# S5 input products as two 96-row matmuls a block, their operands stacked by DMA through DRAM

## The chip, the cores and the metric

The kernel runs on one core of one Trainium2 chip. Its engines are TensorE (PE in the profile, with weight loads as PEld), VectorE (DVE), ScalarE (ACT), GpSimd (POOL) and SyncE (SP); each works through its own queue in order. The metric is device time in microseconds (us), lower is better. Before the change it is 1423.0 us, the median of 3 runs (1422.8 to 1423.98).

## The reference

One decoder block on 256 tokens of width 2048, in float32. After a norm, one large projection (2048 to 9216) feeds two token mixers; gates merge them; a gated MLP with a short convolution follows. The change touches the S5 mixer alone:

```python
uf = u.reshape(bsz, L, 64, 16)                      # 64 groups of 16 channels
abar = exp(lam_re*dt) * (cos(lam_im*dt) + i sin(lam_im*dt))
bu_re = einsum('blgc,gpc->blgp', uf, b_re)          # 16 channels -> 64 states, per group
bu_im = einsum('blgc,gpc->blgp', uf, b_im)
bb = coef * bu                                      # complex, coef from abar and lam
s = associative_scan(affine, (abar, bb))            # along the tokens
y = Re(einsum('blgp,gcp->blgc', s, c)) + d * uf
z = gelu(y); z = z * sigmoid(z @ w_glu + b_glu)     # then @ w_proj_s5
```

The kernel folds `coef` into B, so that a product gives `bb` at once. Each group has its own small product: 16 channels in, 64 complex states out, 256 tokens.

## The kernel before, in words

**Weights in steps.** All dense layers run as 480 weight steps of 512 KB each, in a fixed order: the input projection (144 steps), the GLU (8), the two output projections of the mixers (16 each), the merge (32), the MLP up (176) and down (88). A step's weights are loaded by SP's queue five steps ahead, split two steps ahead by `split_step` into a float32r part `wh` (ACT) and the float32r rest `wl` (DVE), in three buffers each, and multiplied on PE as three products (high by high, high by low, low by high). After a job's last step an epilogue on ACT and DVE takes the sums out of PSUM, of which there are two pairs of banks for this.

**The S5 mixer beside them.** `side_s5` is a generator that is let forward between steps by `side_run`. After each step it may go on while the planner's account of DVE's time is not above that of PE's (`load["dve"] > load["pe"]` ends it), and for at most two pauses. The account is kept by `_dve_cost` and `_pe_cost` (line 84); for a float32r matmul with at least 256 columns the latter books 0.109 for each 256 columns, and half of it where the operand has 32 rows. Before the first GLU step, whatever is left of S5 is let through at once (line 1350); the second mixer, the gated recurrence, follows in the same way with its own deadline.

That is the order in which instructions are written. The framework then fixes the order on each engine before the run: it steps through the program with estimates of durations, takes for each engine the earliest written instruction that it reckons ready and that has a free buffer, and adds the semaphore waits. On the chip each engine follows that order and waits where an input is late.

**A chunk of S5.** The mixer goes through eight chunks (`for ct in range(8)`, line 823) of 8 groups. 32 rows hold two groups' channels, so a chunk has four quarters `q`. `b_place` (line 755, DVE) puts the B of a chunk into a block-diagonal tile `zmat`, one for all chunks. `b_trans` (line 762) transposes its real and imaginary half on PE, splits the result and the chunk's input `u` into high and low parts by `split_pair` (ACT for the high one, DVE for the low one), and leaves all four in one unit `c`: B high, B low, u high, u low, 256 columns each. `b_proj` (line 770) then makes a block of products for two quarters (`pair`): for the real and the imaginary half three products (high by high, high by low, low by high) are summed in PSUM, each on 32 rows; two quarters `a` lie on different rows of the array. That is 12 matmuls a block and 16 blocks in all. The results go to the PSUM tile `bu`, of which there is one.

Behind a block DVE rotates by the tables of angles, scans, rotates back, and `output` (line 783) multiplies by C; its `finish` adds `d * u`. The block of the chunk's second pair is written inside the first pair's turn and the next chunk's first block inside the second pair's turn. `angle_sum` (line 737) runs on POOL for a chunk ahead; `tables` makes sine and cosine on ACT.

Buffers: 26 units of 128 x 1024 (`unit`), which all stages share; six temporaries of 128 x 512 (`tmp`), which epilogues and the S5 tables share; two PSUM banks `ax` for transposes and outputs.

Of the kernel before, what the change touches and what calls it, by code (L numbers as in the profile page):

```python
# [11 lines left out]
F32R = mybir.dt.float32r  # L12
# [5 lines left out]
P = 128  # L18
D = 2048
T = 256  # L20
# [90 lines left out]
def kernel(  # L111
# [8 lines left out]
    A, G, S = nc.scalar, nc.gpsimd, nc.sync  # L120
    load = {"pe": 0.0, "dve": 0.0}
    V, PE = Metered(nc.vector, load, "dve", _dve_cost), Metered(nc.tensor, load, "pe", _pe_cost)
# [13 lines left out]
    dram = ctx.enter_context(tc.tile_pool(name="dram", bufs=1, space=bass.MemoryType.DRAM))  # L136
# [5 lines left out]
    uid = [0]  # L142

    def unit(dt=F32):
        uid[0] += 1
        return up.tile([P, 1024], dt, tag="u4", name=f"u{uid[0]}", bufs=N_UNITS)

    def tmp(dt=F32):
        uid[0] += 1
        return tp.tile([P, 512], dt, tag="tmp", name=f"t{uid[0]}", bufs=6)  # L150
# [13 lines left out]
    def v3(t, n):  # L164
        return t.rearrange("p (a b) -> p a b", a=n)
# [93 lines left out]
    def split_pair(hi, lo, src):  # L259
        A.copy(hi, src)  # L260
        V.tensor_tensor(out=lo, in0=src, in1=hi.bitcast(F32), op=ALU.subtract)
# [9 lines left out]
    def fm_job(wap, c0, nkc, xs, epi, need=None, extra_load=None, wide=False):  # L271


        job = new_job()
        box = {}
        ng = nkc // 4
        for g in range(ng):
            def mm(st, g=g):
                if g == 0:
                    box["ps"] = mm_bank()  # L280
                ps = box["ps"]
                wh, wl = v3(st.wh, 4), v3(st.wl, 4)
                for part in range(2):
                    if part == 1 and st.between is not None:
                        st.between()
                    for j in range(2):
                        cols = slice(j * P, (j + 1) * P)
                        for k in range(4):
                            kc = 4 * g + k
                            xh, xl = xs(kc)  # L290
                            if part == 0 and wide:
                                PE.matmul(ps[:, j, :], wh[:, k, cols], xl, start=kc == 0, stop=False)
                            elif part == 0:
                                PE.matmul(ps[:, j, :T], wh[:, k, cols], xh, start=kc == 0, stop=False)
                                PE.matmul(ps[:, j, :T], wh[:, k, cols], xl, start=False, stop=False)
                            else:
                                PE.matmul(ps[:, j, :T], wl[:, k, cols], xh, start=False, stop=kc == nkc - 1)

            src = wap[0, g * 512:(g + 1) * 512, c0:c0 + 256].rearrange("(k p) c -> p k c", p=P)
            st = weight_step(src, mm, need(g) if need else None, extra_load if g == 0 else None)  # L300
        st.after = (job, lambda: epi(box["ps"]))
        return job
# [163 lines left out]
    u_t = Chunks(8)  # L466
# [64 lines left out]
    u_jobs = [fm_job(w_in, 256 * p, 16, xs_hw, epi_u(p), wide=True) for p in range(4)]  # L531
# [48 lines left out]
    def side_s5():  # L580
# [10 lines left out]
        ax = axbank()  # L591
        PE.transpose(ax[:, 0:64], packB, ident[:64, :64])
        V.tensor_copy(colB, ax[:, 0:64])
        ax = axbank()
        for i in range(3):
            r = P if i < 2 else 96
# [12 lines left out]
        e, s = exp_parts(new, z)  # L609
# [11 lines left out]
        e, s = exp_parts(new, colB[:, 32:64])  # L621
# [4 lines left out]
        e, s = exp_parts(new, la)  # L626
# [87 lines left out]
        for nm, craw, col in (("r", cn[:, 0:512], C_CM), ("i", cn[:, 512:1024], C_CM + 2)):  # L714
# [7 lines left out]
            for half in range(2):  # L722
                ax = axbank()
                for t in range(4):
                    ct = half * 4 + t
# [5 lines left out]
        zmat = cst.tile([P, 2 * P], F32, name="zmat")  # L731
        G.memset(zmat, 0.0)

        bu_in = {}
        angles = {}

        def angle_sum(ct):
            w = angles[ct] = unit()
            q0 = 4 * ct
            w4 = w.rearrange("p (q i j) -> p q i j", q=4, i=16)  # L740
            G.tensor_tensor(out=w4, in0=tabA[:, q0:q0 + 4, :].unsqueeze(3).to_broadcast([P, 4, 16, 16]),
                            in1=tabB[:, q0:q0 + 4, :].unsqueeze(2).to_broadcast([P, 4, 16, 16]), op=ALU.add)
# [12 lines left out]
        def b_place(ct):  # L755
            for i, bb in enumerate((bb_r, bb_i)):
                zv = zmat[:, i * P:(i + 1) * P].rearrange("p (q h c) -> p q h c", q=4, h=2)
                for h in range(2):
                    V.tensor_scalar(out=zv[:, :, h, :], in0=bb[:, 4 * ct:4 * ct + 4, :],
                                    scalar1=cf[:, C_GG + h:C_GG + h + 1], scalar2=None, op0=ALU.mult)  # L760

        def b_trans(ct):
            ax = axbank()
            for i in range(2):
                PE.transpose(ax[:, i * P:(i + 1) * P], zmat[:, i * P:(i + 1) * P], ident)
            c = bu_in[ct] = unit(F32R)
            split_pair(c[:, 0:T], c[:, T:2 * T], ax[:, 0:2 * P])
            split_pair(c[:, 2 * T:3 * T], c[:, 3 * T:4 * T], u_t.at(ct))

        def b_proj(ct, pair):  # L770

            bu = psb.tile([P, 2, 512], F32, tag="bu", name=f"bu{uid[0]}")
            uid[0] += 1
            c = bu_in[ct]
            for i in range(2):
                for j, (hb, hu) in enumerate(((0, 0), (0, 1), (1, 0))):
                    for a in range(2):
                        rows32 = slice(64 * pair + 32 * a, 64 * pair + 32 * a + 32)
                        PE.matmul(bu[:, a, i * T:(i + 1) * T], c[rows32, hb * T + i * P:hb * T + (i + 1) * P],
                                  c[rows32, (2 + hu) * T:(3 + hu) * T], start=j == 0, stop=j == 2)  # L780
            return bu

        def output(ct, rot):
# [36 lines left out]
        bu = b_proj(0, 0)  # L820
        yield
        finish = None
        for ct in range(8):
            rot = []
            sn, cs = tab
            if 1 <= ct < 7:
                angle_sum(ct + 1)
            for pair in range(2):
                b4 = bu.rearrange("p a (c t) -> p a c t", c=2)
                csb = v3(cs, 4)[:, 2 * pair:2 * pair + 2, :].unsqueeze(2).to_broadcast([P, 2, 2, T])  # L830
                snb = v3(sn, 4)[:, 2 * pair:2 * pair + 2, :].unsqueeze(2).to_broadcast([P, 2, 2, T])
                m1, m2 = unit(), unit()
                V.tensor_tensor(out=f4(m1), in0=b4, in1=csb, op=ALU.mult)
                V.tensor_tensor(out=f4(m2), in0=b4, in1=snb, op=ALU.mult)
                yield

                if pair == 0:
                    bu = b_proj(ct, 1)
                elif ct < 7:
                    bu = b_proj(ct + 1, 0)  # L840
                if finish is not None:
                    yield from finish()
                    finish = None
                V.tensor_tensor(out=f4(m1)[:, :, 0, :], in0=f4(m1)[:, :, 0, :], in1=f4(m2)[:, :, 1, :], op=ALU.add)
                V.tensor_tensor(out=f4(m1)[:, :, 1, :], in0=f4(m1)[:, :, 1, :], in1=f4(m2)[:, :, 0, :],
                                op=ALU.subtract)
                for a in range(2):
                    q = 4 * ct + 2 * pair + a
                    for i in range(2):
                        sl = slice(a * 512 + i * T, a * 512 + (i + 1) * T)  # L850
                        V.tensor_tensor_scan(out=m2[:, sl], data0=mag_c[:, q:q + 1].to_broadcast([P, T]),
                                             data1=m1[:, sl], initial=0.0, op0=ALU.mult, op1=ALU.add)
                yield
                if ct < 7 and pair == 0:
                    b_place(ct + 1)
                    yield u_jobs[(ct + 1) // 2]
                    b_trans(ct + 1)
                    yield
                if ct < 7 and pair == 1:
                    tab = yield from tables(ct + 1)  # L860
                V.tensor_tensor(out=f4(m1), in0=f4(m2), in1=csb, op=ALU.mult)
                V.tensor_tensor(out=f4(m2), in0=f4(m2), in1=snb, op=ALU.mult)
                yield
                V.tensor_tensor(out=f4(m1)[:, :, 0, :], in0=f4(m1)[:, :, 0, :], in1=f4(m2)[:, :, 1, :],
                                op=ALU.subtract)
                V.tensor_tensor(out=f4(m1)[:, :, 1, :], in0=f4(m1)[:, :, 1, :], in1=f4(m2)[:, :, 0, :], op=ALU.add)
                rot.append(m1)
                yield
            finish = output(ct, rot)
            yield  # L870
# [346 lines left out]
    for p in range(22):  # L1217
        for half in range(2):
            j = fm_job(w_up, half * NF + 256 * p, 16, xs_x2, epi_up(p, half), need=lambda g: (out_jobs[g], 2), wide=True)
# [184 lines left out]
```

## Time and profile before

| what | value |
|---|---|
| median of 3 runs | 1423.0 us (1422.8 to 1423.98) |
| the profiled execution | 1422.75 us, its span 1420.6 us |
| mean granted TensorE clock | 0.997 |
| busy: PE, PEld, DVE, ACT, POOL | 99%, 83%, 74%, 53%, 3% of the span |
| DMA | 278.58 MB, 196 GB/s mean |
| the 192 S5 input products on PE (`bu<-u`) | 15.6 us busy, from 112.7 to 414.6 us |

The span runs from the first to the last instruction of the profiled execution. "Busy" is the time in which an engine had at least one instruction running; matmuls overlap, so PE's cost of a group is better read from start to start in the timeline. A group's row names the tiles (`out<-in`, numbers left out), the shape, the count, the busy time with the mean of one, and the idle time of the engine just ahead with what ended it. Most rows have line 106, that of the helper which keeps the planner's account, so rows are told apart by their tiles: `bu<-u` are the S5 input products, `ax<-cf,zmat` the transposes of `b_trans`, `u<-ax,u` and `u<-u,u` with 256 float32r columns its splits, `mm` the weight steps.

### The profile page before, as it was taken

To read this page: it belongs to the slowest core of one execution; us is meant where nothing else is said; L and a number is where in the kernel's file an instruction comes from. 1 tells how busy PE (TensorE), PEld (TensorE's weight loads), DVE (VectorE), ACT (ScalarE), POOL (GpSimd) and SP (SyncE) were. 2 spreads that over 40 slices of the span, in tenths; PEclk is the share of its full clock that TensorE was granted. 3 is DMA by queue.
4 is the path that set the end of the run, shared out by engine and by line. 5 is a ranking of instruction groups with operands and counts; after the bars stand their busy time and mean duration, and the time that the engine had idled before them with its cause. 6 is when DMAs were issued, how large, how long until landed. Compare 5 with 4: busy or idle time off the path is not lost.

```text
span 1420.6 us, 20722 instructions
## 1 busy us (share of the span) xinstructions
PE 1403.4 (99%) x8008; PEld 1182.1 (83%) x8008; DVE 1056.9 (74%) x1453; ACT 757.7 (53%) x962; POOL 38.0 (3%) x33
## 2 busy tenths in 40 slices
PE   9999999999999999999999999999999999999997
PEld 7878887877778787888888888888888888888885
DVE  7999989998978968655777777777777775545454
ACT  5455576665655464454555555555555554434343
POOL 1040000000001000000000000000000000000000
PEclk9999999999999999999999999999999999999999
DMA  7865767666767466666666666666666666666653
GB/s 237 219 195 149 218 206 219 202 205 187 210 191 262 154 199 207 220 212 207 193 191 185 188 192 187 186 191 191 185 189 191 188 187 193 201 193 201 194 194 125
DMA packets 215940, 278.58 MB, mean 196 GB/s; under 512 B 19938, under 2 KB 141042, under 8 KB 215841
## 3 DMA queue, kind: packets, MB, share of 16 engines
q1 hardware_dynamic: 198496, 266.57, 60.5%
q10 hardware_dynamic: 17088, 10.49, 2.4%
q8 instruction: 63, 1.03, 0.3%
q14 instruction: 37, 0.30, 0.1%
q0 software_dynamic: 256, 0.19, 0.0%
HBM read 266.73 MB, written 10.49 MB: 195 GB/s over the span
## 4 chain that ended last, share of the span: by engine, by line
PE 95%; DVE 2%; DMA 1%; ACT 1%; issue 0%; POOL 0%; ACTq 0%; DVEq 0%; POOLq 0%
PE mm L106 87%; PE ax L106 7%; DVE u L106 1%; PE bu L106 1%; DMA u<-d 1%; DVE wl L106 1%; DMA u<-in_s_log_dt_dram 0%; ACT wh L256 0%; DVE t L106 0%; PE dummy L106 0%; DVE zmat L106 0%; ACT u L1275 0%; DVE x2g L106 0%; ACT hT L405 0%; ACT t L1259 0%
## 5 line engine op out<-in xcount | busy, mean ns | idle before, releaser
L256 ACT CAST wh<-wr 128x1024 fp32r<-128x1024 f32 x480 | 503.0, 1051 | 587.7 <-PE mm L106 424.2
L106 DVE TENSOR_TENSOR wl<-wr,wh 128x1024 fp32r<-128x1024 f32 x480 | 588.2, 1228 | 304.3 <-ACT wh L256 301.3
L106 PE MATMUL mm<-x2g,wh 128*128 128x512 f32 x1408 | 352.6, 392 | 0.0
L106 PEld LDWEIGHTS mm<-x2g,wh 128*128 128x128 f32 x1408 | 253.3, 189 | 45.3
L106 PE MATMUL mm<-wh,u 128*128 128x512 f32 x1040 | 260.7, 392 | 0.0
L106 PEld LDWEIGHTS mm<-wh,u 128*128 128x128 f32 x1040 | 193.7, 188 | 39.7
L106 PEld LDWEIGHTS mm<-x2g,wl 128*128 128x128 f32 x1408 | 192.0, 190 | 13.6
L106 PE MATMUL mm<-x2g,wl 128*128 128x256 f32 x1408 | 196.4, 282 | 0.0
L106 PE MATMUL mm<-wh,hT 128*128 128x512 f32 x768 | 193.6, 394 | 0.0
L106 PEld LDWEIGHTS mm<-wh,hT 128*128 128x128 f32 x768 | 142.1, 188 | 33.5 <-issue 2.9
L106 PE MATMUL mm<-wl,u 128*128 128x512 f32 x520 | 140.6, 390 | 0.0
L106 DVE TENSOR_TENSOR u<-u,u 128x512 f32<-128x512 f32 (+4 forms) x144 | 114.8, 821 | 0.5
L106 PEld LDWEIGHTS mm<-wl,u 128*128 128x128 f32 x520 | 97.4, 188 | 20.0
L106 PE MATMUL mm<-wl,hT 128*128 128x512 f32 x384 | 102.9, 390 | 0.0
L106 PE MATMUL mm<-hT,wh 128*128 128x512 f32 x384 | 100.4, 401 | 0.8 <-ACT wh L256 0.8
L106 PEld LDWEIGHTS mm<-wl,hT 128*128 128x128 f32 x384 | 72.1, 188 | 15.5
L106 PEld LDWEIGHTS mm<-hT,wh 128*128 128x128 f32 x384 | 69.9, 192 | 14.8 <-ACT wh L256 1.0
L106 DVE SCALAR_TENSOR_TENSOR t<-ub,colC,t 128x256 f32<-128x256 f32 x176 | 73.3, 479 | 0.0
L106 PEld LDWEIGHTS mm<-hT,wl 128*128 128x128 f32 x384 | 52.1, 191 | 4.7 <-DVE wl L106 1.3
L106 PE MATMUL mm<-hT,wl 128*128 128x256 f32 x384 | 54.3, 284 | 0.3 <-DVE wl L106 0.3
L1200 ACT ACTIVATE t<-ub,colC 128x256 f32<-128x256 f32 x88 | 48.0, 593 | 0.0
L106 PE MATMUL ax<-wh,u 128*128 128x512 f32 x176 | 43.3, 389 | 0.0
(186 smaller groups left out, 861.2 us busy)
## 6 DMA issues: line engine op xcount, KB each, us to landing
wr<-in_w_up_dram SPq DMA_DIRECT2D x176, 512.0 KB, 4.5
wr<-in_w_in_dram SPq DMA_DIRECT2D x144, 512.0 KB, 4.4
wr<-in_w_down_dram SPq DMA_DIRECT2D x88, 512.0 KB, 4.7
wr<-in_w_out_dram SPq DMA_DIRECT2D x32, 512.0 KB, 4.2
wr<-in_w_proj_s_dram SPq DMA_DIRECT2D x16, 512.0 KB, 4.0
wr<-in_w_proj_hgrn_dram SPq DMA_DIRECT2D x16, 512.0 KB, 4.8
d<-t ACTq DMA_DIRECT2D x28, 256.0 KB, 4.4
rl<-d SPq DMA_DIRECT2D x16, 256.0 KB, 4.3
```

Source lines behind the costliest of these rows:

```text
L106: return fn(*args, **kw)
L256: A.copy(st.wh, st.w)
L1200: A.activation(out=av, in_=ub[:, a, 0:T], func=AF.Identity, scale=conv_col(0, n), bias=colC[:, 264 + n:265 + n])
```

## The change

The three products of a sum are stacked along the rows. The operand tiles `stB` and `stU` (two units of each, taken in turn by chunk parity) hold, for each quarter `q`, 96 rows: B high, B high, B low in one and u high, u low, u high in the other. One matmul with 96 rows then gives the whole sum, so a block is four matmuls instead of twelve, on rows 0 to 95 of the array.

The splits go to two temporaries, `bc` (B high and low) and `uc` (u high and low). Each is stored to a DRAM tile as it is, by a DMA of 256 KB on GpSimd's queue, and read back by three DMAs of 128 KB (32 rows, four quarters, 256 columns), one for each third of the 96 rows, on the same queue.

The placing and splitting of the next chunk is moved from the first pair's turn, behind the scans, to the top of the chunk, ahead of the first pair's rotation. That of chunk 0 stays where it is.

```diff
-        bu_in = {}
+        stB, stU = ([unit(F32R) for _ in range(2)] for _ in range(2))
...
-            c = bu_in[ct] = unit(F32R)
-            split_pair(c[:, 0:T], c[:, T:2 * T], ax[:, 0:2 * P])
-            split_pair(c[:, 2 * T:3 * T], c[:, 3 * T:4 * T], u_t.at(ct))
+            bc, uc = tmp(F32R), tmp(F32R)
+            split_pair(bc[:, 0:T], bc[:, T:2 * T], ax[:, 0:2 * P])
+            split_pair(uc[:, 0:T], uc[:, T:2 * T], u_t.at(ct))
+
+            for src, dst, parts in ((bc, stB, (0, 0, 1)), (uc, stU, (0, 1, 0))):
+                uid[0] += 1
+                d = dram.tile([P, 512], F32R, name=f"st{uid[0]}")
+                G.dma_start(out=d, in_=src)
+                dv = d.rearrange("(q r) (s t) -> r s q t", q=4, s=2)
+                for j, part in enumerate(parts):
+                    G.dma_start(out=v3(dst[ct % 2], 4)[32 * j:32 * j + 32, :, :], in_=dv[:, part, :, :])
 
         def b_proj(ct, pair):
...
-            c = bu_in[ct]
-            for i in range(2):
-                for j, (hb, hu) in enumerate(((0, 0), (0, 1), (1, 0))):
-                    for a in range(2):
-                        rows32 = slice(64 * pair + 32 * a, 64 * pair + 32 * a + 32)
-                        PE.matmul(bu[:, a, i * T:(i + 1) * T], c[rows32, hb * T + i * P:hb * T + (i + 1) * P],
-                                  c[rows32, (2 + hu) * T:(3 + hu) * T], start=j == 0, stop=j == 2)
+            sB, sU = v3(stB[ct % 2], 4), v3(stU[ct % 2], 4)
+            for a in range(2):
+                qq = 2 * pair + a
+                for i in range(2):
+                    PE.matmul(bu[:, a, i * T:(i + 1) * T], sB[0:96, qq, i * P:(i + 1) * P], sU[0:96, qq, :],
+                              start=True, stop=True)
             return bu
...
             if 1 <= ct < 7:
                 angle_sum(ct + 1)
+            if ct < 7:
+                b_place(ct + 1)
+                yield u_jobs[(ct + 1) // 2]
+                b_trans(ct + 1)
+                yield
             for pair in range(2):
...
                 yield
-                if ct < 7 and pair == 0:
-                    b_place(ct + 1)
-                    yield u_jobs[(ct + 1) // 2]
-                    b_trans(ct + 1)
-                    yield
                 if ct < 7 and pair == 1:
```

## The prediction

> **What bounds the kernel now.** I read the page's busy line and digits first, then the busy time by stretch.
>
> ```profile
> span 1420.6 us, 20722 instructions
> PE 1403.4 (99%) x8008; PEld 1182.1 (83%) x8008; DVE 1056.9 (74%) x1453; ACT 757.7 (53%) x962; POOL 38.0 (3%) x33
> PE   9999999999999999999999999999999999999997
> DVE  7999989998978968655777777777777775545454
> PEclk9999999999999999999999999999999999999999
> 112.00:134.00 22.00, 21.85 (x116) 17.79 (x115) 21.32 (x26) 10.58 (x14) 0.00 (x0) 1.00 0.53 157
> 134.00:179.00 45.00, 45.00 (x246) 36.80 (x245) 44.93 (x57) 24.16 (x28) 3.02 (x1) 1.00 0.67 199
> 179.00:447.00 268.00, 268.00 (x1383) 215.66 (x1383) 244.44 (x289) 166.08 (x187) 8.94 (x5) 1.00 0.66 203
> 447.00:560.00 113.00, 111.41 (x1249) 90.67 (x1248) 89.40 (x143) 64.18 (x117) 5.89 (x2) 1.00 0.63 209
> ```
>
> The last four rows are stretches: length, then busy time of PE, weight loads, DVE, ACT and POOL, the granted clock, the DMA share and GB/s. PE is full at full clock from end to end, so a microsecond taken out of PE's stream comes off the end, as long as no other engine makes PE stand. The rows also say who could: the S5 products lie between 112 and 415 us, and in the first part of that, 112 to 179, DVE is as full as PE (66.25 of 67 us); afterwards it has room (244.44 of 268).
>
> **Removed: 192 row-tiled products.** The next rows are PE's stream around one block of S5 products (twelve matmuls, one pair of groups), and around a stretch of plain 256-column matmuls; the first column is the start.
>
> ```profile
> 394.15 1.07 PE L106 MATMUL mm<-wl,hT 128*128 128x512 f32 x4
> 395.15 0.98 PE L106 MATMUL bu<-u 32*128 32x256 f32 x12
> 396.06 2.12 PE L106 MATMUL mm<-wh,hT 128*128 128x512 f32 x8
> 398.02 1.08 PE L106 MATMUL mm<-wl,hT 128*128 128x512 f32 x4
> 398.93 1.98 PE L106 MATMUL mm<-wh,hT 128*128 128x512 f32 x8
> 400.75 1.07 PE L106 MATMUL mm<-wl,hT 128*128 128x512 f32 x4
> ...
> 450.69 1.11 PE L106 MATMUL mm<-u,wl 128*128 128x256 f32 x8
> 451.64 1.55 PE L106 MATMUL mm<-u,wh 128*128 128x512 f32 x6
> ```
>
> Without a block, four `wl` matmuls take 398.93 - 398.02 = 0.91 us from start to start and eight `wh` 400.75 - 398.93 = 1.82. With a block between, the same two take 396.06 - 394.15 = 1.91 and 398.02 - 396.06 = 1.96. So a block costs PE 1.00 + 0.14 = 1.14 us, its twelve matmuls and the changes into and out of the 32-row form together; 16 blocks cost 18.2 us.
>
> **Added on PE: 64 whole-array products.** No row shows 96 rows by 128 columns with fp32r. The nearest is the plain 256-column matmul, each with its own weights: (451.64 - 450.69) / 8 = 0.119 us. Four of them are 0.48 us, the lower bound of a block (no change of form is left in it). The upper bound is that each waits for its weight load:
>
> ```profile
> L106 PEld LDWEIGHTS mm<-wh,hT 128*128 128x128 f32 x768 | 142.1, 188 | 33.5 <-issue 2.9
> ```
>
> at 188 ns, four are 0.75 us. The 256-column row has loads of that length too and hides them, so I take 0.50. The gain is 16 x (1.14 - 0.50) = 10.2 us, with bounds 16 x (1.14 - 0.75) = 6.2 and 16 x (1.14 - 0.48) = 10.6.
>
> **Added: the trip through DRAM.** Each chunk issues eight DMAs from POOL's queue: two stores of 256 KB and six loads of 128 KB, where the splits used to write straight into the operand. The loads wait on POOL for the store to land. POOL's own DMAs occur only at the start; the others stand for the landing:
>
> ```profile
> 2.59 0.51 POOL L209 DMA_DIRECT2D u<-in_s_b_glu_dram  x1
> 3.59 0.58 POOL L213 DMA_DIRECT2D u<-in_conv_w_dram  x1
> d<-t ACTq DMA_DIRECT2D x28, 256.0 KB, 4.4
> u<-d SPq DMA_DIRECT2D x12, 256.0 KB, 6.0
> u<-in_s_log_dt_dram POOLq DMA_DIRECT2D x1, 0.2 KB, 4.3
> u<-in_conv_w_dram POOLq DMA_DIRECT2D x2, 64.0 KB, 6.0
> ```
>
> One issue is 0.55 us and one landing 4.4 to 6.0. From split to products: a store (0.55 + 4.4 to 6.0), three load issues (1.65), a landing (4.4 to 6.0) make 11.0 to 14.2 us; I take 12.6. If u's half stands in front on the queue, up to 2.2 us of its issues are added.
>
> [...]
>
> In all, 64 issues keep POOL 35 us over some 300 us; behind them on its queue stand only the angle sums, which POOL works off far ahead. The added 10.5 MB are 35 GB/s on top of 203 at a share of 0.66; the first 60 us ran at 0.82. ACT and DVE do the same four splits a chunk as before, into two of the six temporaries. I cost these at nothing: if a temporary is held 6 us too long, a job's epilogue waits, and PE has the second PSUM pair, eight steps (22 us), meanwhile.
>
> **From the second chunk on the trip is hidden.** The split is moved to the top of the chunk ahead, before that chunk's second block. The rows give the distances:
>
> ```profile
> 353.21 0.98 PE L106 MATMUL bu<-u 32*128 32x256 f32 x12
> 371.95 0.97 PE L106 MATMUL bu<-u 32*128 32x256 f32 x12
> 395.15 0.98 PE L106 MATMUL bu<-u 32*128 32x256 f32 x12
> ```
>
> Chunk 6's second block starts at 371.95, chunk 7's first at 395.15: 23.2 us, and the transposes now come a little before 371.95. The trip with its split is about 15.2 us (12.6 + 2.6, next part). What it costs if that cover goes is the third rival.
>
> **The first chunk has nothing to hide it.** Its placing isn't moved, and its products are written right behind it:
>
> ```profile
> 109.57 0.38 PE L106 MATMUL ax<-cf,zmat 128*128 128x128 f32 x2
> 112.68 0.98 PE L106 MATMUL bu<-u 32*128 32x256 f32 x12
> 112.16 0.42 DVE L106 TENSOR_TENSOR u<-ax,u 128x256 fp32r<-128x256 f32 x1 [0.40 <-ACT u L260]
> 124.18 1.22 DVE L106 TENSOR_TENSOR wl<-wr,wh 128x1024 fp32r<-128x1024 f32 x1
> 128.03 1.07 PE L106 MATMUL mm<-wl,hT 128*128 128x512 f32 x4
> 112.00:130.00 18.00, 1.96 (x24) 1.58 (x24) 10.92 (x16) 1.67 (x4) 0.00 (x0) 1.00 0.50 143
> ```
>
> The transposes end at 109.95, the split ends at 112.58, 2.6 us later, and the products start at 112.68; with the trip they can start at 125.2. The framework's scheduler fixes each engine's order beforehand by what it reckons to be ready, so I expect weight matmuls in front of these products, and no 12.6 us hole in PE. DVE pays instead. The last row is the S5 tiles alone: 10.92 us of DVE's 18. About 1.2 us of it (three splits) needs no products: 9.7 us in 18, so a wait of 12.6 us leaves DVE 6.8 us short; the next chunk's placing and split (about 1.8 us), now written ahead, fill part of it: 5.0 are left. DVE had 0.75 us to spare until 179 us, and its late S5 work goes before the splits of later weights. What PE has in hand is the time from a split's end to its use: the one at 124.18 ends at 125.40, and by the three buffers its matmuls are those at 128.03, 2.6 us. So PE loses 5.0 - 2.6 = 2.4 us. To this comes the error of the planned order: where the products are placed earlier than the data land, PE stands; I put 2.6 us there, from bounds of 0 and 12.6 (placed as written). Together 5.0 us, bounds 0 and 14.
>
> **The seam at the end of S5.** The code's planner books a product with 32 rows at half of 0.109, any other at 0.109: a block falls from 0.654 to 0.436, 16 blocks by 3.5, and S5 is let forward only as far as PE's booked time. A weight step is booked at 2.6, so S5 ends 1.3 steps later against the weights, and the GLU matmuls behind (448.87 on) need its last output; the gated recurrence starts later too, with its own deadline. PE was busy 111.41 of 113 us there. I put 1.0 us, bounds 0 and 3.
>
> **Sum.** The profiled execution took 1422.75 us, 2.15 more than its span, and the median of the runs is 0.25 above it. 1422.75 - 10.2 + 5.0 + 1.0 = 1418.55; on the median 1418.8. I say **1419**, with 1416 to 1422 as this case's own spread.
>
> **Rivals.** (A) The first chunk costs nothing: the order is well planned and DVE catches up. Against it stands DVE's 66.25 of 67 us. 1423 - 10.2 + 0.5 = 1413. (B) PE stands through the whole first trip, because the products are placed where they are written: 1423 - 10.2 + 13 + 1 = 1427, slower; it decides once the loss passes 12 us. For it speaks that on PE the products stood as written. (C) The trip outgrows its cover in every chunk: from about 21 us on (two landings of 9 us, or issues of 3 us) the first block of each later chunk waits; 3 us over in seven chunks is 21: 1423 - 10.2 + 6 + 21 = 1440. Nothing before shows POOL issuing while DVE is full; the issue rows are from the idle start. [...] (D) The products don't get cheaper as meant, each waiting for its weights: 1423 - 6.2 + 6 = 1423.
>
> **Chances and range.** The forecast has 0.45, A 0.15, B 0.17, C 0.14, D 0.09. About 0.2%, 2.8 us, can be told from no change. Faster (below 1420.2): 0.31 of the forecast and A, 0.46. Same: 0.14 of the forecast, D, and 0.06 of B, 0.29. Slower (above 1425.8): the other 0.11 of B and C, 0.25. The range, 1412 to 1429, takes in A, B and D, and leaves out C.
>
> **What would show it.** On PE a block of four 96-row products should add about 0.5 us to the matmuls around it. In the first chunk, the first block should start near 125 us with weight matmuls in front; a hole of over 5 us before it in PE's waits is B. POOL's issues should stay near 0.55 us and landings near 5; if PE waits for DMA before the first block of several chunks, C. DVE waits should move to 113 to 125, and PE waits for `wl` follow. If PE's total idle time does not grow and the time is near 1413, my loss at the first chunk was wrong.

## The result and the profile after

The changed kernel takes **1429.25 us** (median of six runs, 1428.0 to 1436.06) against 1423.16 for the kernel before beside it: a ratio of 1.0052, interval 1.0032 to 1.0073. It is half a per cent slower, where 1419 was forecast. The execution that was profiled is the longest of the six, 1436.06 us, so beside its page I read a second profile of the same kernel (span 1426.9 us, experiment 1); where the two differ I go by the second.

The busy line of the first page and its row on the loads of the stacked operand (size, median time from issue to landing):

```profile
span 1434.3 us, 20593 instructions
PE 1400.3 (98%) x7880; PEld 1182.0 (82%) x7880; DVE 1061.5 (74%) x1453; ACT 760.5 (53%) x964; POOL 73.9 (5%) x97
...
u<-st POOLq DMA_DIRECT2D x48, 128.0 KB, 6.5
```

PE runs 128 matmuls fewer, but the span is longer: PE now stands. Where it stands is seen by stretches (second profile; length, then busy time of PE, weight loads, DVE, ACT and POOL, granted clock, DMA share, GB/s):

```profile
112.00:134.00 22.00, 20.57 (x95) 16.77 (x94) 11.54 (x11) 9.08 (x10) 9.04 (x14) 1.00 1.05 285
134.00:160.00 26.00, 20.97 (x91) 15.09 (x90) 26.00 (x33) 10.98 (x12) 1.13 (x2) 0.87 0.47 138
160.00:179.00 19.00, 19.00 (x102) 16.38 (x101) 18.41 (x20) 8.87 (x10) 5.19 (x7) 1.00 0.95 255
179.00:447.00 268.00, 262.87 (x1290) 215.02 (x1290) 254.24 (x299) 169.79 (x190) 37.23 (x46) 1.00 0.78 228
447.00:530.00 83.00, 82.00 (x1109) 66.55 (x1108) 68.82 (x99) 45.09 (x66) 5.31 (x2) 1.00 0.67 218
530.00:560.00 30.00, 25.71 (x130) 21.20 (x128) 17.81 (x40) 17.40 (x51) 0.00 (x0) 0.89 0.46 146
```

Before, PE stood 0.15 us from 112 to 179, nothing to 447 and 1.59 to 560 (the lengths less the busy times in the prediction's first fence): 1.7 us. Now it stands 6.5, 5.1 and 5.3, together 16.9 (rounded), and the clock is below one twice. DVE, which was full from 112 to 134, is idle for 10.5 us there. What PE waits for between 100 and 560 us (in total, times, longest):

```profile
PE mm L106 <- DVE wl L106: 7.2, 3, 4.2
PE ax L106 <- DVE u L106: 4.3, 1, 4.3
PE mm L106 <- ACT wh L256: 2.1, 1, 2.1
PE bu L106 <- DMA u<-st: 1.4, 1, 1.4
PE ax L106 <- POOL u L907: 1.0, 1, 1.0
PE bu L106 <- issue: 0.7, 1, 0.7
```

Only 1.4 us of it is the new operand itself. Most of the rest is split weights that come late (`wl`, `wh`) and one long wait behind the gated recurrence (`ax` for DVE).

The gain is there too. The rows around one stacked block (second profile):

```profile
402.47 1.07 PE L106 MATMUL mm<-wl,hT 128*128 128x512 f32 x4
403.38 0.64 PE L106 MATMUL bu<-u,u 96*128 96x256 f32 x4
403.86 2.00 PE L106 MATMUL mm<-wh,hT 128*128 128x512 f32 x8
405.70 1.07 PE L106 MATMUL mm<-wl,hT 128*128 128x512 f32 x4
```

From block to next matmul are 0.48 us, and the eight `wh` behind it take 1.84 instead of 1.82: 0.50 us a block, where it was 1.14. Sixteen such blocks give 10.2 us. So some 16 us are lost elsewhere. The two profiles account for them: from 112 to 560 us PE stands 15.1 us more. From 60 to 112 it stands 2.6 us less, mostly because a wait of 2.33 us at 101.50 in the kernel before isn't there. And its busy time falls by 6.7 us (1403.4 to 1396.7) instead of 10.2; part of that is the lower clock behind the long waits (2.5 us behind the first, last section). With half a microsecond elsewhere this makes the 6.3 us between the spans, 1420.6 and 1426.9.

### The profile page after: what moved, and what is told of

The parts are those of the page before. It is cut to its first block, busy times and chain, and to the rows that moved or that the text cites. A ratio compares the mean times of both kernels' runs of the same rounds, so it can differ in the third digit from the quotient of the medians.

```text
span 1434.3 us, 20593 instructions
## 1 busy us (share of the span) xinstructions
PE 1400.3 (98%) x7880; PEld 1182.0 (82%) x7880; DVE 1061.5 (74%) x1453; ACT 760.5 (53%) x964; POOL 73.9 (5%) x97
## 4 chain that ended last, share of the span: by engine, by line
PE 65%; ACT 1%; DVE 1%; issue 0%
PE mm L106 59%; PE ax L106 6%; ACT t L1007 0%; DVE wl L106 0%; ACT wh L256 0%; DVE u L106 0%; ACT u L1003 0%; ACT u L1281 0%; ACT L350 0%; DVE x2g L106 0%; DVE rss L106 0%; ACT t L1265 0%; DVE fin L106 0%; ACT x2g L1164 0%; DVE o_rs L106 0%
## 5 line engine op out<-in xcount | busy, mean ns | idle before, releaser
L106 PEld LDWEIGHTS mm<-wh,hT 128*128 128x128 f32 x768 | 145.1, 191 | 31.0 <-issue 1.2
L106 DVE TENSOR_TENSOR u<-u,u 128x512 f32<-128x512 f32 (+3 forms) x136 | 108.3, 822 | 0.6
```

The source lines that it names most:

```text
L106: return fn(*args, **kw)
```

## The experiments

Each run's ratio is to runs of the kernel before beside it (1422.6 to 1423.6 us). The table collects the medians; the two columns differ only in what the planner books for a stacked block.

| S5's input products | block booked at 0.436 | block booked at 0.654, as before |
|---|---|---|
| all 16 blocks stacked, with the trip | 1428.7 (1.0026 to 1.0056) | 1427.6 (1.0019 to 1.0045) |
| chunk 0 in the old form, 14 stacked | 1426.3 (1.0018 to 1.0037) | 1420.5 (0.9971 to 0.9992) |
| chunks 0 to 2 in the old form, 10 stacked | 1429.2 (1.0026 to 1.0054) | **1418.4 (0.9954 to 0.9980)** |
| 16 blocks of the same matmuls, no trip | 1419.7 (0.9966 to 0.9986) | 1416.9 (0.9938 to 0.9968) |

**1. The same kernel again.**

> The changed kernel as it is, a second profile. Theory: two stalls of TensorE carry the loss and stand in every execution: one between 120 and 160 us (DVE's idle time in the first chunk, 12.9 of 22 us in the profile already seen, comes out as some 10 us of TensorE's waits for wl and for the S5 operand), one of 4 to 5 us near 546 us, ahead of proj_hgrn. Then the time is 1428 to 1430 and both stalls are in this profile too. Rival (chance): the 7 us by which the profile already seen lies above the median are one of those two stalls; then one of them is missing here. Rival (transfers): waits for the DMA of S5's operand differ from profile to profile, and the stacked blocks at 208 and 242 us show waits of another length.

Measured: 1428.7 us. Both stalls are there. Between 134 and 160 PE stands 5 us, around one wait of 4.21 us; near 540 it waits 4.29 us. The waits for the stacked operand do vary: 4.0 us in two places in the longest execution, 1.4 in one place here. They are the smaller part. Where the first chunk's time goes shows in three engines' order of work (start, duration; the wait before an operation stands in brackets):

```profile
108.51 1.13 POOL L773 DMA_DIRECT2D st<-t  x2 [20.82 <-DVE t L106]
112.84 4.34 POOL L776 DMA_DIRECT2D u<-st  x8 [1.34 <-DMA st<-t]
119.22 0.54 POOL L776 DMA_DIRECT2D u<-st  x1 [2.04 <-DMA u<-st]
...
124.40 0.74 PE L106 MATMUL bu<-u,u 96*128 96x256 f32 x4 [1.43 <-DMA u<-st]
...
122.28 1.23 DVE L106 TENSOR_TENSOR wl<-wr,wh 128x1024 fp32r<-128x1024 f32 x1 [1.50 <-ACT wh L256]
127.20 1.23 DVE L106 TENSOR_TENSOR wl<-wr,wh 128x1024 fp32r<-128x1024 f32 x1 [3.69 <-ACT wh L256]
129.92 1.22 DVE L106 TENSOR_TENSOR wl<-wr,wh 128x1024 fp32r<-128x1024 f32 x1 [1.49 <-ACT wh L256]
131.06 2.35 DVE L106 TENSOR_TENSOR u<-bu,u 128x1024 f32<-128x1024 f32 x2
```

The first block starts at 124.40, with weight matmuls ahead of it and a wait of 1.43 us. It ends at 125.14. DVE's first use of it, the rotation, is six microseconds later, at 131.06: the planned order has two splits of weights ahead of it, each waiting for ScalarE's cast. In the kernel before, the block ended at 113.66 and the rotation followed at once:

```profile
114.25 2.35 DVE L106 TENSOR_TENSOR u<-bu,u 128x1024 f32<-128x1024 f32 x2
```

Why the order has it so late is taken up in experiment 10. In the changed kernel DVE is full from 131 on, and the next splits come late: PE's 4.21 us at 149.67.

**2. The booking, the first chunk, and both.** Experiment 2 changes one price:

```diff
-    ... * (0.5 if args[1].shape[0] == 32 else 1.0)
+    ... * {32: 0.5, 96: 1.5}.get(args[1].shape[0], 1.0)
```

> Only the planner's price of a 96-row product is changed, so that a block is booked at 0.654 us as it was before the change (it is 0.436 in the changed kernel). Theory (booking): the gated recurrence ends past its deadline because 16 blocks are booked 3.5 us lower and S5 and the recurrence are let forward later against the weights; with the old booking the stall near 546 us goes from over 4 us to under 1, the time falls by 6 to 8 us to 1421 to 1423. Rival (lateness): the recurrence is late because S5 as a whole is late after its first chunk; then the booking moves nothing there, and the time stays at 1427 to 1430.

Measured: 1427.6 us, not to be told from the changed kernel, as the rival had it. But the stall near 540 did go: PE is busy 29.88 of 30 us from 530 to 560. The time came back elsewhere: PE stands 2.8 us instead of 1.0 from 447 to 530 and 5.6 instead of 5.1 from 179 to 447 (nine waits for split weights of 0.15 to 1.3 us), and it is busy for 1.8 us longer in all (1398.5 against 1396.7). The theory's mechanism is there; its price, 6 to 8 us, is not.

Experiment 3 puts chunk 0 back into the old form:

```diff
+            if ct == 0:
+                c = first["c"] = unit(F32R)
+                split_pair(c[:, 0:T], c[:, T:2 * T], ax[:, 0:2 * P])
+                split_pair(c[:, 2 * T:3 * T], c[:, 3 * T:4 * T], u_t.at(ct))
+                return
...
+            if ct == 0:
+                # twelve 32-row products a block, as in the kernel before
```

> Only chunk 0 goes back to the old form (both splits into one operand tile, two blocks of twelve 32-row products, no trip through DRAM); chunks 1 to 7 stay stacked. Theory: DVE's idle time between 112 and 134 us falls from 12.9 to under 3 us and the step ledger loses its rise of some 13 us at 126 to 240 us, but the stall near 546 us stays, and 14 blocks give 9 us: 1420 to 1423. Rival (lateness): with the first chunk in time the stall near 546 us goes too: 1413 to 1416. Rival (every trip costs): later chunks make the loss, the time stays above 1425.

Measured: 1426.3 us, where the last rival put it. Yet what the theory said of the places holds: DVE is busy 19.03 of the 22 us from 112 to 134 again, and the stall near 540 stays, with a wait of 4.3 us. The first block is in time again (108.27 to 109.24), but DVE's rotation of it stands at 121.10 only, though no trip lies between the two.

Experiment 4 has both edits.

> Both edits: chunk 0 in the old form, and a block booked at 0.654 us. Theory: both stalls go, what is left is the gain of 14 blocks (14 x 0.6 = 8 to 9 us) less what the queue of POOL costs in chunk 3 (about 2): 1415 to 1417, faster than before. Rival (every trip costs): above 1422.

Measured: 1420.5 us, 5.8 under experiment 3 and 7.1 under experiment 2. Neither edit alone brings the gain out; each removes a stall that the other one leaves or moves. It is 0.2% faster than before, but 3.5 to 5.5 us short of what I expected.

**3. The parts alone.** Experiment 5 has only the move, in the kernel before:

```diff
+            if ct < 7:
+                b_place(ct + 1); yield u_jobs[(ct + 1) // 2]; b_trans(ct + 1); yield
             for pair in range(2):
...
-                if ct < 7 and pair == 0:
-                    b_place(ct + 1) ...
```

> The kernel before with only the move: the next chunk's placing, transposes and splits stand at the top of the chunk, ahead of its second block; the products keep the old 32-row form and there is no trip through DRAM. Theory (trip): the move alone costs nothing, the first chunk has no idle time of DVE: 1422 to 1424. Rival (order): four more splits and two placings stand ahead of chunk 0's own work while DVE is full, so the move alone costs 2 to 4 us: 1425 to 1427.

Measured: 1423.0 us, ratio 0.9996 (0.9987 to 1.0006). The move costs nothing.

Experiment 6 has the stacked matmuls without the trip, experiment 9 the same with the old booking; the products read the first 96 rows of the tile that the splits write:

```diff
-            (the eight DMAs of the trip)
...
-    PE.matmul(..., sB[0:96, qq, i * P:(i + 1) * P], sU[0:96, qq, :], ...)
+    PE.matmul(..., c[0:96, i * P:(i + 1) * P], c[0:96, (qq % 2 + 2) * T:(qq % 2 + 3) * T], ...)
```

> The changed kernel without its trip: no DMA of GpSimd, the products are the same 96-row instructions but read the first 96 rows of the tile that the splits write, as soon as the splits are done. What it leaves out: the stacking, so the sums of S5's input products are wrong, the work is the same. Theory (trip and DVE): with no wait for the operand the gain of 16 blocks (9.8 us) comes out less what DVE cannot follow in the chunks where it was full (66.25 of 67 us up to 179 us: 5 blocks, 3 us) and less a seam of 2 to 6 us at the end of the gated recurrence: 1414 to 1420. Rival (seam only): if the lower booking alone makes the loss, this kernel has it too and is not faster than 1422. Rival (trip only): 1413.

> The kernel without the trip (96-row products that read the splits' own tile, stacking left out, so the sums of S5's input products are wrong) and a block booked at 0.654 us as before the change. Theory: the seam at the end of the gated recurrence (4.3 us of waiting and a clock of 0.5 for some 5 us in the run without the trip) comes from the booking alone when nothing else is late; with the old booking it goes and the time is 1412 to 1415. Rival: what the run without the trip did not gain is DVE that cannot follow; then the waits only move to another place and the time stays at 1418 to 1420.

Measured: 1419.7 and 1416.9 us. Even where nothing waits for a trip, 3.7 and 6.6 of the 10.2 us come out. The rows of experiments 6 and 9 (each 112 to 179, 179 to 447, 447 to 560):

```profile
112.00:179.00 67.00, 67.00 (x344) 56.11 (x344) 66.42 (x80) 36.19 (x43) 2.85 (x1) 1.00 0.65 193
179.00:447.00 268.00, 266.30 (x1314) 217.45 (x1313) 247.31 (x296) 168.25 (x191) 7.99 (x5) 1.00 0.68 209
447.00:560.00 113.00, 108.06 (x1221) 88.21 (x1220) 87.41 (x140) 59.31 (x111) 5.76 (x2) 0.97 0.59 194
```

```profile
112.00:179.00 67.00, 64.82 (x321) 53.78 (x321) 65.22 (x82) 33.82 (x41) 2.84 (x1) 0.97 0.64 187
179.00:447.00 268.00, 267.16 (x1320) 218.07 (x1319) 248.87 (x295) 171.04 (x193) 7.72 (x5) 1.00 0.67 208
447.00:560.00 113.00, 110.85 (x1247) 90.29 (x1246) 90.95 (x143) 62.01 (x114) 5.09 (x2) 1.00 0.62 204
```

With the old booking PE stands 5.2 us, 3.5 more than before. (The execution profiled is the longest of its four: its span is 3.3 us under that of the kernel before, the median 6.6, so the stretches can't be added up to the median.) With the low booking it stands 4.9 us in the last stretch alone, with the clock at 0.97. That stretch is the seam at the end of S5 and of the gated recurrence. Both theory and rival of experiment 9 were half right: the seam went, 2.8 us came of it, and some of the waiting moved ahead.

Experiment 10 is experiment 9 with all 64 DMAs carried out, into tiles that nobody reads.

> As the run before, but all 64 DMAs of the trip are carried out from the same tile, into operand tiles that nobody reads (the products still read the splits' own tile, so the sums are wrong in the same way). Theory (contention): the transfers and GpSimd's issues themselves delay the weights (ScalarE waits for the weights' DMA were 0.8 us between 112 and 450 us before and are 11 to 21 in the stacked runs) and lengthen DVE's work beside them; 3 to 6 us over the run without the trip. Rival (data wait only): without a product that waits for the data the trip costs nothing, within 1 us of it.

Measured: 1417.7 us, 0.8 above experiment 9, with intervals that overlap. The contention theory's 3 to 6 us did not come: no cost of the transfers and issues is seen above the noise, as the prediction had it. ScalarE's waits for the weights' DMA, which had led me to the theory (0.8 us before, 11.2 in experiment 1), are no measure of the loss. Experiments 10 and 11, both faster than before, have 3.7 and 16.1 us of them (112 to 450 us).

Experiments 2 and 10 differ in little but that the products wait for the data (the stores also leave from temporaries in the one and from the splits' tile in the other; that was not tried apart). So the waiting, with whatever the held temporaries add, costs 1427.6 - 1417.7 = 9.9 us.

The profile of experiment 10 also says where this cost does not lie:

```profile
112.00:134.00 22.00, 22.00 (x100) 18.28 (x100) 15.08 (x18) 10.35 (x13) 9.55 (x15) 1.00 1.14 283
134.00:160.00 26.00, 20.80 (x88) 14.91 (x87) 26.00 (x33) 11.08 (x12) 1.13 (x2) 0.87 0.53 157
179.00:447.00 268.00, 267.72 (x1330) 219.50 (x1330) 252.98 (x302) 171.96 (x194) 44.03 (x46) 1.00 0.78 234
```

```profile
126.25 1.22 DVE L106 TENSOR_TENSOR wl<-wr,wh 128x1024 fp32r<-128x1024 f32 x1 [1.49 <-ACT wh L256]
127.39 2.35 DVE L106 TENSOR_TENSOR u<-bu,u 128x1024 f32<-128x1024 f32 x2
```

No product waits for a trip here, and the first block is done at 109.44. Yet DVE idles for 6.9 us up to 134, and PE stands 5.2 us from 134 to 160 with the same low clock as in the changed kernel (5.0 there). So that stall comes without a data wait, too. Up to 447, on the other hand, PE stands 0.3 us, where it stands 5.6 in experiment 2 (262.39 of 268 us busy), with DVE as busy in both (252.98 and 253.50).

The rotation is late in every run in which chunk 1 goes through DRAM, whether chunk 0 waits or not (experiments 2, 4 and 8, left out of the table, have 5.9, 11.8 and 13.8 us):

| run | first block ends | DVE's rotation | behind it by |
|---|---|---|---|
| kernel before | 113.66 | 114.25 | 0.6 us |
| 5 (move alone) | 114.22 | 116.64 | 2.4 |
| 9 (no trip) | 114.78 | 117.17 | 2.4 |
| 11 (chunks 0 to 2 old) | 114.50 | 116.94 | 2.4 |
| changed kernel (experiment 1) | 125.14 | 131.06 | 5.9 |
| 3 (chunk 0 old, chunk 1 by DRAM) | 109.24 | 121.10 | 11.9 |
| 7 (first trip early, see below) | 117.26 | 131.05 | 13.8 |
| 10 (trip that nobody waits for) | 109.44 | 127.39 | 18.0 |

Chunk 1's splits and DMAs are written ahead of this rotation, by the move. The move without the trip (experiments 5, 6 and 9) doesn't put it off like this; with the trip it does. How is not shown, and the trip without the move was not tried. The rotation reads nothing of chunk 1, so the planner's reckoning of when things are ready, or the 26 shared units, of which the operand tiles take four, are the candidates; neither was tried.

**4. The first trip earlier.** Chunk 0 is placed, transposed, split and sent ahead of the two C tables, all 16 blocks stacked; experiment 8 adds the old booking.

```diff
-        CT = {} ...          (both C tables)
...
+        b_place(0); yield; yield u_jobs[0]; b_trans(0); yield
+        CT = {} ...          (both C tables)
         angle_sum(0)
```

> The changed kernel with chunk 0 placed, transposed, split and sent on its trip some 25 us earlier, ahead of the two C tables, so that its operand lies ready when the angle tables are; all 16 blocks stacked. Theory: DVE's idle time in the first chunk falls from over 10 us to under 3, as with the old form, and two more blocks are gained: 1 us under the run with chunk 0 in the old form, 1424 to 1426; the stall near 540 us stays. Rival: the first chunk's loss comes from the order of DVE's queue behind it and stays: 1428.

> The early first trip together with a block booked at 0.654 us as before the change. Theory: the two costs cover each other, and only both edits together bring the gain out: 1 us under the run with the old first chunk and the old booking, 1418 to 1420. Rival (booking does nothing when the first chunk is in time): as the early trip alone, 1424 to 1426.

Measured: 1435.2 and 1426.0 us, both far from what the theory expected; the second is where the rival had it. The edit brought a stall of its own (experiment 7):

```profile
104.88 6.15 DVE L106 TENSOR_SCALAR u<-u,cf 128x512 f32<-128x512 f32 x4
106.13 3.82 POOL L723 TENSOR_TENSOR u<-u 128x1024 f32<-128x1024 f32 x2
110.30 1.97 PE L106 MATMUL ax<-cf,u 128*128 128x128 f32 x8 [4.42 <-DVE u L106]
```

The four multiplications of the C tables take 6.15 us beside GpSimd's angle sums, and PE waits 4.42 us for them. In experiment 1 two of them stand beside the angle sums, which ran from 78.08 for 9.61 us there, and two do not:

```profile
83.73 4.25 DVE L106 TENSOR_SCALAR u<-u,cf 128x512 f32<-128x512 f32 x2
97.31 0.88 DVE L106 TENSOR_SCALAR u<-u,cf 128x512 f32<-128x512 f32 x2
```

Their times are 4.25 and 0.88 us. The rows show the delay, not what causes it. As a test of what the first chunk costs in time these runs are inconclusive, since two things changed at once. But they do show that an early operand isn't enough: the first block of experiment 7 is done at 117.26, and the rotation still stands at 131.05.

**5. Stacked only where DVE has room.** `if ct == 0` of experiment 3 becomes `if ct < 3`, with the old booking in experiment 11 and the low one in experiment 12.

> Chunks 0 to 2 in the old form, chunks 3 to 7 stacked with their trip, a block booked at 0.654 us; the whole of S5's input is right. Theory: the stacked form pays where DVE has room (from 179 us on 244.44 of 268 us were busy); 10 blocks give 6 us, the trips of five chunks cost 2 to 3: 1418.5 to 1420, not slower than the run with only chunk 0 in the old form (1420.5) though it stacks four blocks fewer. Rival: the gain goes with the number of stacked blocks and the cost is the first chunk's alone: 1422.

> Chunks 0 to 2 in the old form and chunks 3 to 7 stacked as in the run before, but a 96-row product booked at 0.109 us as in the changed kernel, so that a stacked block is booked at 0.436 us. Theory (booking): ten stacked blocks are booked 2.2 us too low, the gated recurrence ends past its deadline and the wait of some 4 us near 540 us with the lower clock behind it comes back: 2 to 5 us over the run with the old booking, 1420.5 to 1423.5. Rival (lateness): with no early trip nothing is late, the recurrence ends in time and the price in the planner does not matter: 1418 to 1419.

Measured: 1418.4 and 1429.2 us. Ten stacked blocks give 5.1 us, fourteen gave 2.2; the intervals of the two ratios overlap (0.9954 to 0.9980, 0.9971 to 0.9992), so that ten do better than fourteen is likely and not shown. Experiment 11 is faster than the kernel before, by 0.33%. PE doesn't stand in it or in experiment 12 up to 179 us. The rows of experiment 11 behind that and then those of experiment 12:

```profile
179.00:447.00 268.00, 266.50 (x1325) 216.76 (x1324) 245.91 (x292) 166.96 (x191) 39.48 (x46) 1.00 0.79 231
447.00:560.00 113.00, 110.59 (x1245) 89.97 (x1244) 89.99 (x143) 61.58 (x113) 5.14 (x2) 1.00 0.62 203
```

```profile
179.00:447.00 268.00, 262.72 (x1292) 213.62 (x1291) 245.60 (x288) 164.21 (x185) 34.93 (x46) 1.00 0.78 227
447.00:560.00 113.00, 108.16 (x1227) 87.10 (x1227) 85.85 (x137) 62.49 (x114) 5.81 (x2) 0.97 0.60 195
```

In experiment 11 PE stands 3.9 us, 2.2 more than before; the ten blocks give 6.4, and 4.2 are left, where the medians show 5.1 and the spans of the two profiles 2.9. In experiment 12 the price in the planner alone takes 10.8 us away. PE stands 4.8 us in the last stretch, with the low clock, and 5.3 us ahead of it, and is busy for 4.1 us longer in all (1401.5 against 1397.4). The theory had said 2 to 5 us. That a lower price brings the seam's stall back is shown. Why it also costs 3.8 us between 179 and 447 is not: the planned order is another one there, and I have not taken it apart. It is not that DVE has more to do: it is busy for 245.60 us there against 245.91.

## Why the prediction was wrong

**Right:** the block (0.50 us, the gain of 10.2). The start of the first block (125.2 forecast, 124.40 and 126.37 seen), with weight matmuls ahead of it and no hole over 5 us, which rules out rival B. GpSimd's issues (0.55 us in the mean for the loads, 0.57 for the stores, first page). The move alone and the traffic alone at nothing (experiments 5 and 10). Rival B's time, 1427 us, lies close to the measured one by luck: its hole in PE isn't there. Rival C did not come: PE waited for the stacked operand once or twice, not in every chunk, and no row shows the 3 us an issue that C named. Landings were longer than the bounds said (6.5 and 6.8 us for the loads), and the cover still held them but for one or two blocks. Rival D is ruled out by the block.

**In all.** The forecast was 10.2 us gained, 5.0 lost to the first trip and 1.0 at the seam. Taken one after the other by the medians, the runs give: the same matmuls with no trip and the old booking 6.6 us gained (experiment 9), the low booking 2.8 lost (6), the trip 9.0 lost (1). In the other order the trip costs 10.7 and the booking 1.1.

**"The first chunk", sized 5.0 us, and "From the second chunk on the trip is hidden", at nothing.** These are the steps that failed. Together they are the trip, and it measured 9.0 us (1428.7 against 1419.7 without the trip) or 10.7 (1427.6 against 1416.9), within the bounds of 0 and 14, but about twice the size. Three things in them were wrong.

First, I let DVE go on with S5 as soon as the first products were done, 12.6 us late. In the changed kernel its rotation stands 5.9 us behind them, and DVE is idle for 10.5 us, where I had put 6.8 less what fills it. The table of experiment 10 shows that the rotation is late whenever the next chunk's trip is written ahead of it, also where the first block doesn't wait: the second chunk's trip is hidden from PE, but not from DVE. The stall of some 5 us around 145 us stands in experiment 10 too, where no product waits.

Second, I let the debt end with 2.6 us of slack, once. In the changed kernel PE stands 5.1 us more between 179 and 447, in three waits for split weights from 207 to 275 us. DVE has 10 us more to do there (254.24 of 268 us, before 244.44). It seemed that the debt is paid there bit by bit, but this is not shown, and two runs speak against it: with DVE at 252.98 us experiment 10 stands 0.3 us, and with DVE at 245.60 experiment 12 stands 5.3. What is shown is that the products' wait for their data costs some 10 us in all (experiments 2 and 10, the temporaries included). By which late operations it does so between 179 and 447 stays open.

Third, later trips were not free. Taking chunks 1 and 2 back too (experiment 4 to 11) gave up four blocks, 2.6 us by the rows, and lost no time: the median is 2.1 us lower, within the noise.

**"The seam at the end of S5", sized 1.0 us, bounds 0 and 3.** The step named the cause, 3.5 us less booked and a recurrence that starts later, but not its size. From the second profile, with S5 late too:

```profile
531.55 4.18 PE L106 MATMUL ax<-u,u 128*128 128x128 f32 x36
538.58 0.17 DVE L106 TENSOR_SCALAR rsv<-o_ss 128x16 f32<-128x16 f32 x1 [5.43 <-ACT t L1007]
542.76 1.96 PE L106 MATMUL ax<-cf,u 128*128 128x128 f32 x7 [4.29 <-DVE u L106]
```

The recurrence's last matmuls, 36 in a row, are done against the deadline, its sums of squares on ScalarE and the norm on DVE follow with too few weight matmuls planned to cover them, and PE waits 4.29 us and then runs at half clock (0.50 from 542 to 546 us). The lower price costs 2.8 us without the trip, 5.8 with chunk 0 in the old form and 10.8 with chunks 0 to 2, where only a part is the seam. In the changed kernel itself the old price gives only 1.1, within the noise: the stall goes, and the time is lost elsewhere. So these terms don't add, and the sum had added them.

**What the sum left out:** that a faster PE needs its other engines faster too. The prediction said itself that DVE was as full as PE up to 179 us, and then counted the whole 10.2 as gain. With no trip and the old booking 6.6 of it came out, with 3.0 us of standing up to 447 in that profile (2.2 of them in one wait for DVE at 151.91), where the kernel before stood 0.15.

## What to carry to other kernels

Where another engine is nearly as full, count a cheaper matmul's gain only as far as that engine can follow: here 6.6 of 10.2 us came out with no trip and the old booking, and ten blocks stacked where DVE had room did no worse than fourteen. When work is written ahead to hide a delay, look in the profile at the first consumer of the old work too, and not only at the engine that waits for the data: here DVE's rotation stood 6 us behind its block in the changed kernel and up to 18 in a run in which nobody waits for the operand. A delay can cost much more than the wait that the profile puts down to it (here the trip cost 9.0 us, and PE waited 1.4 us for the operand), so measure it by a run that does the same work and doesn't wait. Where an order is planned from booked costs, a lower price is a change by itself: here the same ten stacked blocks ran at 1418.4 or 1429.2 us by that number alone.

## What was not expected of the hardware

**A long wait of PE cost more than the wait.** Stretches of two microseconds each around the wait at 145 us (second profile), and the matmuls behind it:

```profile
144.00:146.00 2.00, 1.34 (x8) 0.34 (x6) 2.00 (x4) 0.50 (x2) 0.00 (x0) 1.00 0.00 0
148.00:150.00 2.00, 0.33 (x1) 0.34 (x2) 2.00 (x3) 1.46 (x2) 0.00 (x0) 0.50 0.00 0
152.00:154.00 2.00, 2.00 (x6) 1.61 (x5) 2.00 (x2) 0.63 (x1) 0.00 (x0) 0.50 0.77 231
```

```profile
149.67 2.07 PE L106 MATMUL mm<-wl,hT 128*128 128x512 f32 x4 [4.21 <-DVE wl L106]
151.54 3.52 PE L106 MATMUL mm<-wh,hT 128*128 128x512 f32 x8
154.89 1.09 PE L106 MATMUL mm<-wl,hT 128*128 128x512 f32 x4
```

After 4.21 us of idle time the granted clock is 0.50, and the two groups take 2.07 and 3.52 us instead of 1.07 and 1.98: 2.5 us more on top of the wait, until 154.9. The same stands behind the wait of 4.29 us that ends at 542.76 (0.50 from 542 to 546). A shorter wait did it once, in the kernel before (2.33 us at 101.50, then 0.59 and 0.56 up to 106), and another left the clock at 1.00 (2.07 us at 206.89, second profile; 1.00 over 179 to 447). Behind the wait at 145 us the clock came back after 5.2 us of work (149.67 to 154.89). What sets its fall and its return isn't shown. The prediction priced every wait at its bare length.
